# A two-layer decoder trunk on one core: q, k and two gate/up halves laid out with a gap, and the last pieces in two PSUM banks

## The chip, the core and the metric

The kernel runs on one core of a Trainium2 chip. The core has five engines that this document names as the profile does: PE (matrix multiply; its weight loads are shown as PEld), DVE (vector), ACT (scalar), POOL and SP. SP and ACT also issue the transfers between memory and the on-chip buffer SBUF; matrix results land in PSUM, which has eight banks. The metric is the time of one execution in microseconds, as the median of several runs.

## The reference

Two layers over 256 positions of width 1024, all in float32. Each layer is a token mixer (16 heads of 64; forgetting attention in layer 0, block attention with a learned relative bias in layer 1), a SwiGLU feed-forward of width 2816, and a gated per-layer input; a final RMSNorm gives the output of 256 x 1024.

```python
for i in range(DEPTH):                       # DEPTH = 2
    u = _rmsnorm(h, attn_norm_g[i])
    if i % 2 == 0:                           # forgetting attention
        proj = u @ fox_w_in[j]               # q, k, v and 16 gate columns
        ...
        o = _fox_attention(q, k, v, log_f)
        h = h + _merge_heads(o) @ fox_w_o[j]
    else:
        proj = u @ moba_w_in[j]              # q, k, v
        ...
        o = _moba_attention(q, k, v, rel_bias_table)
        h = h + _merge_heads(o) @ moba_w_o[j]
    u = _rmsnorm(h, ffn_norm_g[i])
    gu = u @ ffn_w_in[i]
    h = h + (jax.nn.silu(gu[..., :D_FF]) * gu[..., D_FF:]) @ ffn_w_out[i]
    gate = jax.nn.sigmoid(_rmsnorm(h, ple_norm_g[i]) @ ple_w_gate[i])
    h = h + gate * (p[i] @ ple_w_up[i])
return _rmsnorm(h, final_norm_g)
```

## The kernel before

**Weights come as halves.** The host cuts all weights into 216 "halves" of 128 x 1024 float32 (512 KB), in the order of their use, in the tensor `w`. `half` (L115) takes the next one: a transfer on SP's queue into a tile `raw` (six slots), a copy on ACT that rounds it to the PE's short float format (`whi`, L137), and a subtraction on DVE that leaves the rest (`wlo`, L138). `whi` and `wlo` are rings of six slots each. Every product is made of three matmuls (`mm3`, L80 to L84): high by high, high by low, low by high.

**Which operand is loaded.** In the products `pq` (q and k, `project`, L385) and `gu` (gate and up, `step` in `up`, L503), the half's blocks of 128 columns are the loaded weights and the activations `g` (tiles of `Norm`, high and low, 256 positions) are the moving operand. `blocks` (L141) cuts such a half into its eight blocks. In `v`, `wo`, `fo` and `pg` it is the other way round: activations are loaded, and a half is streamed in pieces of 512 columns.

**Places of the blocks.** A slot starts at a multiple of 64 elements (`LINE`). `blocks` puts the halves 16 elements behind that (`APART`). With `entry` set, `half` puts the first two blocks of the low part another 8 elements further (`FURTHER`), and the rest a `LINE` behind; this takes two subtractions (L129) instead of one. `up` asks for an entry for the gate's half of every even f from 4 on, and for the up half of f = 2 (L518).

**Order.** Each engine's instructions are put in order when the program is built. In `attention`, the j-th pair of heads goes through `project(j, 0)`, `scores(j - 1)` (`sp`), `transposes(j - 2)` (`pp`), `project(j, 1)` and `values(j - 2)` (`po`), so that a half of `pq` (24 matmuls) stands between other work. In `ffn`, f = 0 and 1 are done together over k, with the transposes `tp` of the second half of the residual between k = 2 and 3; then f = 2 with `spread` (`pr`) behind its first half; from f = 4 on, four halves (96 matmuls) follow on two halves of `fo` (`down`).

**The forget gate's weights.** In layer 0, `fox_bias` (L271) splits `wf32` into `fh` and `fl`, two tiles of their own of 4 KB per partition, zeroed once on POOL.

**The end.** In layer 1 `ple` (L596) closes with the final norm. The second half of the columns of `pg` (512 to 1023) is made for the first 128 positions (t = 0) with 512-wide matmuls, and for the last 128 (t = 1) in two pieces of 256 columns, both in one PSUM bank. Each piece goes through `part` (L644): a sigmoid on ACT, two DVE operations that add the gated input to `h`, and a square with its sum on ACT. For each t, POOL makes the scale from the sums (L670, L671); ACT scales the first 512 columns and sends them from its own queue, DVE finishes the other 512, and SP sends them. t = 0 is scaled and sent before t = 1's second piece.

```python
for i in range(2):
    for k in range(KT):
        c0 = (k % 2) * HC + i * S
        tokens(bks[1][t][:, i * S:(i + 1) * S], nm.k(k), t, ...)
    if i == 0:
        part(t, 0)
```

Of the kernel before, what the change touches and what calls it, by code (L numbers as in the profile page):

```python
# [32 lines left out]
P = 128  # L33
S = 256
# [23 lines left out]

ENTRY = 2
FURTHER = 8  # L60


@with_exitstack
def trunk(ctx: ExitStack, tc: tile.TileContext, x, xt, pt, w, wf, cst, pick, gains, gf, bf, rel, hot, rvm, out):
# [50 lines left out]
    def half(at=0, entry=0):  # L115


        i = state["next"]
        state["next"] += 1
        raw = work.tile([P, HW], F32, tag="raw", bufs=RAW, name=f"raw{i}")  # L120
        hi = work.tile([P, HW + LINE], F32R, tag="whi", bufs=6, name=f"whi{i}")[:, at:at + HW]
        lt = work.tile([P, HW + 2 * LINE], F32R, tag="wlo", bufs=6, name=f"wlo{i}")
        lo = lt[:, at:at + HW]
        if entry:
            nc.sync.dma_start(raw, w[i])
            nc.scalar.activation(hi, raw, AF.Copy)  # L126
            ats = [(at + FURTHER, 0, entry), (at + LINE, entry, HW)]
            for a, c0, c1 in ats:
                nc.vector.tensor_tensor(lt[:, a + c0:a + c1], raw[:, c0:c1], f32(hi[:, c0:c1]), op=ALU.subtract)  # L129
            return hi, [lt[:, a + k * P:a + (k + 1) * P] for a, c0, c1 in ats for k in range(c0 // P, c1 // P)]  # L130
        parts = 2 if i < 2 else 1
        for q in range(parts):
            c = slice(q * HW // parts, (q + 1) * HW // parts)
            if i == 0 and q == 1:
                nc.sync.dma_start(hx[:, 1], xt[:, 1])
            nc.sync.dma_start(raw[:, c], w[i][:, c])
            nc.scalar.activation(hi[:, c], raw[:, c], AF.Copy)  # L137
            nc.vector.tensor_tensor(lo[:, c], raw[:, c], f32(hi[:, c]), op=ALU.subtract)  # L138
        return hi, lo

    def blocks(entry=False):  # L141

        hi, lo = half(APART, ENTRY * P if entry else 0)
        hi = [hi[:, k * P:(k + 1) * P] for k in range(KT)]
        return hi, lo if entry else [lo[:, k * P:(k + 1) * P] for k in range(KT)]

# [95 lines left out]
    for t in (fh, fl):  # L242
        nc.gpsimd.memset(f32(t)[:, :, :, H:], 0.0)

    def split(hi, lo, src):
# [25 lines left out]
    def fox_bias(nm):  # L271


        split(fh[:, :, :, 0:H], fl[:, :, :, 0:H], wf32.unsqueeze(2).to_broadcast([P, KT, 4, H]))
        pf = bank("pf")
# [59 lines left out]
    def attention(layer, nm, mid, early, nf):  # L335
# [159 lines left out]
    def ffn(layer, nm, filler, np_):  # L495
# [3 lines left out]
        def up(fs):  # L499
# [96 lines left out]
    def ple(layer, nm, ut, nx):  # L596

        def gate(bk, t, c0, c1):
            at = slice(c0, c1)
            sg = work.tile([P, HC], F32, tag="t2k", bufs=3, name=f"pgt{layer}_{t}_{c0}")[:, 0:c1 - c0]  # L600
            nc.scalar.activation(sg, bk[:, c0 % HC:(c1 - 1) % HC + 1], AF.Sigmoid, scale=nm.col[:, t:t + 1])
            nc.vector.tensor_tensor(sg, sg, ut[:, t, at], op=ALU.mult)
            nc.vector.tensor_tensor(h[:, t, at], h[:, t, at], sg, op=ALU.add)

        bks = [[bank(f"pg{layer}_{hf}_{t}") for t in range(2)] for hf in range(2)]
# [26 lines left out]
        def square(t, i, c0, c1):  # L632

            sq = work.tile([P, HC], F32, tag="t2k", bufs=3, name=f"sqf{t}_{i}")
            nc.scalar.activation(sq[:, 0:c1 - c0], h[:, t, c0:c1], AF.Square, scale=D ** -0.5,
                                 accum_out=ss[:, t, i:i + 1])
# [7 lines left out]
        def part(t, i):  # L644
            c0 = HC + i * S
            gate(bks[1][t], t, c0, c0 + S)
            square(t, 1 + i, c0, c0 + S)
            if i == 0:
                nc.vector.tensor_tensor(ms[:, t, 1:2], ms[:, t, 0:1], ss[:, t, 1:2], op=ALU.add)
                nc.vector.tensor_tensor(ys[:, t, HC:HC + S], h[:, t, HC:HC + S], gb[:, HC:HC + S], op=ALU.mult)  # L650

        def rows(t, c0, c1, queue):
            queue.dma_start(out[t * P:(t + 1) * P, c0:c1], ys[:, t, c0:c1])

        for t in range(2):
            if t == 0:
                for c in range(4):
                    pair_unit(bks[1], c, wts[c], nm.k, (t,))
                part(t, 0)
            else:  # L660
                for i in range(2):
                    for k in range(KT):
                        c0 = (k % 2) * HC + i * S
                        tokens(bks[1][t][:, i * S:(i + 1) * S], nm.k(k), t, [w[:, c0:c0 + S] for w in wts[k // 2]],
                               k == 0, k == KT - 1)
                    if i == 0:
                        part(t, 0)
            part(t, 1)
            r = col[:, t:t + 1]
            nc.gpsimd.tensor_tensor(r, ss[:, t, 2:3], ms[:, t, 1:2], op=ALU.add)  # L670
            nc.gpsimd.tensor_tensor(r, r, nhalf[:, 0:1], op=ALU.pow)  # L671
            nc.scalar.activation(ys[:, t, 0:HC], ys[:, t, 0:HC], AF.Copy, scale=r)
            rows(t, 0, HC, nc.scalar)
            nc.vector.scalar_tensor_tensor(ys[:, t, HC + S:D], h[:, t, HC + S:D], r, gb[:, HC + S:D],
                                           op0=ALU.mult, op1=ALU.mult)
            nc.vector.tensor_scalar(ys[:, t, HC:HC + S], ys[:, t, HC:HC + S], r, None, op0=ALU.mult)
            rows(t, HC, D, nc.sync)

    for layer in range(2):
# [8 lines left out]
        nm = Norm(3) if layer == 0 else None  # L688
        ple(layer, np_, got[0], nm)


# [93 lines left out]
```

## Time and profile before

| | us |
|---|---|
| median of 3 runs | 674.04 (673.87 to 674.23) |
| the profiled execution's own time | 674.86 |
| its span, first to last instruction | 673.0 |
| PE busy in the span | 661.4 |
| DVE busy | 453.2 |
| ACT busy | 385.8 |
| mean granted clock of PE | 0.997 |

Times in the profile count from the first instruction. Matmuls overlap in the records (one is shown with its whole way through the array), so the time that one takes up on PE is read from the start of one to the start of the next. `gu<-g,whi` reads: the tile `gu` is written from `g` and `whi`; `L82` is the line of the program; `x704` counts instructions. A name after `<-` in square brackets is what ended an idle time. An arrow in the list of waits reads "waited for".

### The profile page before, as it was taken

Reading aid. Unit: us, or ns where it says so; the run is one execution under the profiler, and the core shown is the slowest. Engines: PE = TensorE matmul, PEld = TensorE weight load, DVE = VectorE, ACT = ScalarE, POOL = GpSimd, SP = SyncE. Lnnn points to the kernel's source line nnn. Section 1 sums busy time; section 2 is a strip of 40 time slices with the busy share of each in tenths; the row PEclk is TensorE's granted clock in tenths of the full one; section 3 lists DMA queues with packets and bytes.
Section 4 is the critical chain, followed back from the end, with each engine's and each line's share of the span. In section 5 each row is a group of like instructions: output and inputs, shape, how many; then the busy total and the mean of one; then the engine's idle time right before and its main releaser. Section 6 shows DMA issues by size and latency. Waiting matters only on the chain.

```text
span 673.0 us, 11820 instructions
## 1 busy us (share of the span) xinstructions
PE 661.4 (98%) x4620; PEld 607.0 (90%) x4620; DVE 453.2 (67%) x804; ACT 385.8 (57%) x697; POOL 10.0 (1%) x26
## 2 busy tenths in 40 slices
PE   8999999999999999999999999999999999999994
PEld 6889998999999999998889999889999999999884
DVE  5688775676666666666676888765766666666673
ACT  6876675564444444547666766655544444454663
POOL 2000000000000000000000000000000000000000
PEclk9999999999999999999999999999999999999998
DMA  8976334456555556555585533353755555565401
GB/s 277 384 279 237 126 127 129 153 170 207 193 196 195 199 188 208 193 197 174 185 286 199 172 127 126 107 175 107 241 195 193 197 197 188 188 212 195 173 1 62
DMA packets 37063, 123.78 MB, mean 184 GB/s; under 512 B 4288, under 2 KB 7056, under 8 KB 37008
## 3 DMA queue, kind: packets, MB, share of 16 engines
q1 hardware_dynamic: 36128, 121.35, 53.3%
q10 hardware_dynamic: 848, 1.68, 0.7%
q8 instruction: 36, 0.59, 0.3%
q14 instruction: 19, 0.16, 0.1%
q0 software_dynamic: 32, 0.01, 0.0%
HBM read 121.94 MB, written 4.22 MB: 187 GB/s over the span
## 4 chain that ended last, share of the span: by engine, by line
PE 92%; DMA 3%; ACT 2%; DVE 1%; issue 1%; SPq 0%; POOLq 0%; DVEq 0%; POOL 0%; ACTq 0%
PE gu L83 12%; PE gu L82 12%; PE gu L84 12%; PE fo L83 6%; PE fo L82 6%; PE fo L84 6%; PE pq L82 4%; PE pq L84 4%; PE pq L83 4%; DMA raw<-w 2%; PE wo L82 2%; PE wo L84 2%; PE wo L83 2%; PE pg L82 2%; PE pg L84 2%; PE pg L83 2%
## 5 line engine op out<-in xcount | busy, mean ns | idle before, releaser
L138 DVE TENSOR_TENSOR wlo<-raw,whi 128x1024 fp32r<-128x1024 f32 (+1 forms) x198 | 239.7, 1214 | 141.1 <-ACT whi L137 140.9
L137 ACT ACTIVATE whi<-raw 128x1024 fp32r<-128x1024 f32 (+1 forms) x198 | 207.2, 1050 | 159.3 <-PE gu L83 46.7
L82 PE MATMUL gu<-g,whi 128*128 128x256 f32 x704 | 195.5, 278 | 0.0
L84 PE MATMUL gu<-g,wlo 128*128 128x256 f32 x704 | 195.1, 277 | 0.0
L83 PE MATMUL gu<-g,whi 128*128 128x256 f32 x704 | 195.1, 277 | 0.0
L82 PEld LDWEIGHTS gu<-g,whi 128*128 128x128 f32 x704 | 132.6, 188 | 0.8
L83 PEld LDWEIGHTS gu<-g,whi 128*128 128x128 f32 x704 | 132.3, 188 | 0.7
L84 PEld LDWEIGHTS gu<-g,wlo 128*128 128x128 f32 x704 | 132.2, 188 | 0.0
L82 PE MATMUL pq<-g,whi 128*128 128x256 f32 x256 | 73.9, 289 | 0.0
L84 PE MATMUL pq<-g,wlo 128*128 128x256 f32 x256 | 71.8, 280 | 0.0
L83 PE MATMUL pq<-g,whi 128*128 128x256 f32 x256 | 71.7, 280 | 0.0
L82 PE MATMUL fo<-whi,fh 128*128 128x512 f32 x176 | 68.9, 391 | 0.0
L83 PE MATMUL fo<-wlo,fh 128*128 128x512 f32 x176 | 68.7, 390 | 0.0
L84 PE MATMUL fo<-whi,fl 128*128 128x512 f32 x176 | 68.5, 389 | 0.0
L82 PEld LDWEIGHTS pq<-g,whi 128*128 128x128 f32 x256 | 48.1, 188 | 1.0 <-ACT vhi L373 0.6
L84 PEld LDWEIGHTS pq<-g,wlo 128*128 128x128 f32 x256 | 48.7, 190 | 0.0
L83 PEld LDWEIGHTS pq<-g,whi 128*128 128x128 f32 x256 | 48.4, 189 | 0.0
L246 ACT ACTIVATE fh<-sg 128x256 fp32r<-128x256 f32 x44 | 18.2, 418 | 48.5 <-DVE sg L533 48.5
L129 DVE TENSOR_TENSOR wlo<-raw,whi 128x256 fp32r<-128x256 f32 (+1 forms) x40 | 26.0, 688 | 22.8 <-ACT whi L126 22.8
L84 PEld LDWEIGHTS fo<-whi,fl 128*128 128x128 f32 x176 | 33.1, 188 | 7.1
L82 PEld LDWEIGHTS fo<-whi,fh 128*128 128x128 f32 x176 | 33.1, 188 | 6.3
L83 PEld LDWEIGHTS fo<-wlo,fh 128*128 128x128 f32 x176 | 33.1, 188 | 6.0
(146 smaller groups left out, 967.1 us busy)
## 6 DMA issues: line engine op xcount, KB each, us to landing
raw<-w SPq DMA_DIRECT2D x214, 512.0 KB, 3.3
d<-d SPq DMA_DIRECT2D x4, 768.0 KB, 7.8
bias<-d SPq DMA_DIRECT2D x4, 512.0 KB, 5.2
raw<-w SPq DMA_DIRECT2D x4, 256.0 KB, 5.2
h<-x ACTq DMA_DIRECT2D x2, 512.0 KB, 5.3
hx<-xt SPq DMA_DIRECT2D x3, 256.0 KB, 5.1
p<-pt SPq DMA_DIRECT2D x2, 256.0 KB, 3.5
end<-gf SPq DMA_DIRECT2D x1, 512.0 KB, 4.4
```

What stands on the lines that cost most here:

```text
L82: mm(o, ah, bh, start=start, stop=False, skip_group_check=True)
L83: mm(o, ah, bl, start=False, stop=False, skip_group_check=True)
L84: mm(o, al, bh, start=False, stop=stop, skip_group_check=True)
L129: nc.vector.tensor_tensor(lt[:, a + c0:a + c1], raw[:, c0:c1], f32(hi[:, c0:c1]), op=ALU.subtract)
L137: nc.scalar.activation(hi[:, c], raw[:, c], AF.Copy)
L138: nc.vector.tensor_tensor(lo[:, c], raw[:, c], f32(hi[:, c]), op=ALU.subtract)
L246: nc.scalar.activation(hi, src, AF.Copy)
```

## The change

- **Gap.** A new `gapped` makes a half whose first block is followed by 56 unused columns (`GAP` = 64 - 8). High and low part both start 24 elements behind the slot's start, so the first block lies 8 elements further than with `blocks`, and the other seven lie as with `blocks`, one `LINE` on. The host puts the gap into `w`, so one transfer, one copy and one subtraction of 1080 columns do it. All rows of `w` are 1080 columns long for that, and the other halves take the first 1024.
- **Where.** `gapped` is used in `project` for all but the first three halves of each layer; in `up` for the gate's half of f = 0, where block 3 (the first behind the transposes) is put first, and for the up half of f = 2. The entry of L518 stays for f = 4, 6, and so on.
- **Room.** The slots of `raw`, `whi` and `wlo` grow (`raw` and `whi` by 256 bytes per partition). `fh` and `fl` give up their own tiles and take a slot of the rings.
- **The end.** The two last pieces have a bank each (`pgl`). The halves of the last four `pg` products are laid 48 elements into their slots (`AHEAD`). Both pieces of each t are multiplied with the gain on DVE as they come. Row block t = 0 is scaled on ACT alone, in two parts placed behind the last sigmoid and the last square, and leaves as one transfer of 512 KB on SP's queue; for t = 1 ACT scales the first 512 columns and DVE the other 512, and each is sent as before.

```diff
+GAP = LINE - FURTHER
+WW = HW + GAP
+AHEAD = 48
...
+    def gapped(first=0):
+        i = state["next"]
+        state["next"] += 1
+        raw = work.tile([P, HW + LINE], F32, tag="raw", bufs=RAW, name=f"raw{i}")
+        at = slice(APART + FURTHER, APART + FURTHER + WW)
+        ht, lt = (work.tile([P, HW + 2 * LINE], F32R, tag=n, bufs=6, name=f"{n}{i}")[:, at] for n in ("whi", "wlo"))
+        nc.sync.dma_start(raw[:, 0:WW], w[i])
+        nc.scalar.activation(ht, raw[:, 0:WW], AF.Copy)
+        nc.vector.tensor_tensor(lt, raw[:, 0:WW], f32(ht), op=ALU.subtract)
+        cs = [bool(n) * GAP + n * P for n in (_entered(first).index(k) for k in range(KT))]
+        return [[t[:, c:c + P] for c in cs] for t in (ht, lt)]
...
-    fh, fl = (one.tile([P, KT, 4, 32], F32R, name=n) for n in ("fh", "fl"))
...
+        fh, fl = (work.tile([P, HW + 2 * LINE], F32R, tag=t, bufs=6, name=n)[:, 0:HW].rearrange(
+            "p (k r c) -> p k r c", k=KT, r=4) for n, t in (("fh", "whi"), ("fl", "wlo")))
...
         def project(j, a):
-            hi, lo = blocks()
+            hi, lo = gapped() if 2 * j + a > 2 else blocks()
...
-                wts = {f: (blocks(), blocks()) for f in fs}
+                wts = {f: (blocks() if f else gapped(3), blocks()) for f in fs}
...
-                wt = blocks(a == 1 if fs[0] == 2 else a == 0 and fs[0] % 2 == 0)
+                if fs[0] == 2 and a:
+                    wt = gapped()
+                else:
+                    wt = blocks(ENTRY if fs[0] % 2 == 0 and a == 0 and fs[0] > 2 else ())
...
-        wts = [half() for _ in range(4)]
+        wts = [half(AHEAD) for _ in range(4)]
...
+        lb = (bks[1][1], bank("pgl"))
+        for i in range(2):
+            for k in range(KT):
+                c0 = (k % 2) * HC + i * S
+                tokens(lb[i][:, i * S:(i + 1) * S], nm.k(k), 1, [w[:, c0:c0 + S] for w in wts[k // 2]],
+                       k == 0, k == KT - 1)
+            last = part(1, i, lb[i])
+
+        for ins, c in zip(last, (slice(0, HC), slice(HC, D))):
+            with tc.issue_after(ins.ins):
+                nc.scalar.activation(ys[:, 0, c], ys[:, 0, c], AF.Copy, scale=col[:, 0:1])
+        rows(0, 0, D, nc.sync)
+        nc.scalar.activation(ys[:, 1, 0:HC], ys[:, 1, 0:HC], AF.Copy, scale=col[:, 1:2])
+        rows(1, 0, HC, nc.scalar)
+        nc.vector.tensor_scalar(ys[:, 1, HC:D], ys[:, 1, HC:D], col[:, 1:2], None, op0=ALU.mult)
+        rows(1, HC, D, nc.sync)
...
+def _entered(first):
+    return [first] + [k for k in range(KT) if k != first]
+
+def _gapped(a, first=0):
+    t = a.reshape(P, KT, P)[:, _entered(first)].reshape(P, HW)
+    return np.concatenate([t[:, :P], np.zeros((P, GAP), t.dtype), t[:, P:]], axis=1)
...
+        seq += qk[:3] + [_gapped(a) for a in qk[3:]]
...
+        a[0], a[5] = _gapped(a[0], 3), _gapped(a[5])
...
-    w = np.ascontiguousarray(np.stack(seq))
+    w = np.stack([np.pad(a, ((0, 0), (0, WW - a.shape[1]))) for a in seq])
```

More of the change, by code (lines that the diff above doesn't have):

```diff
@@ L119, in half @@
         state["next"] += 1
[L120 to L123, printed above, removed]
+        raw = work.tile([P, HW + LINE], F32, tag="raw", bufs=RAW, name=f"raw{i}")
+        ht, lt = (work.tile([P, HW + 2 * LINE], F32R, tag=n, bufs=6, name=f"{n}{i}") for n in ("whi", "wlo"))
+        hi, lo = ht[:, at:at + HW], lt[:, at:at + HW]
         if entry:
-            nc.sync.dma_start(raw, w[i])
-            nc.scalar.activation(hi, raw, AF.Copy)
+            nc.sync.dma_start(raw[:, 0:HW], w[i][:, 0:HW])
+            nc.scalar.activation(hi, raw[:, 0:HW], AF.Copy)
             ats = [(at + FURTHER, 0, entry), (at + LINE, entry, HW)]
@@ L139, in half, with blocks @@
         return hi, lo
[L141 to L145, printed above, removed]
+    def blocks(entry=()):
+        hi, lo = half(APART, len(entry) * P)
+        return [[t[k] if isinstance(t, list) else t[:, k * P:(k + 1) * P] for k in range(KT)] for t in (hi, lo)]
+    def gapped(first=0):
+        i = state["next"]
+        state["next"] += 1
+        raw = work.tile([P, HW + LINE], F32, tag="raw", bufs=RAW, name=f"raw{i}")
+        at = slice(APART + FURTHER, APART + FURTHER + WW)
[5 more added lines that the diff above has]
+        return [[t[:, c:c + P] for c in cs] for t in (ht, lt)]
     class Norm:
@@ L641, in ple, with part @@
             nc.vector.tensor_tensor(ys[:, t, 0:HC], h[:, t, 0:HC], gb[:, 0:HC], op=ALU.mult)
[L642 to L644 removed]
+        wts = [half(AHEAD) for _ in range(4)]
+        def part(t, i, bk):
             c0 = HC + i * S
[L646 to L647 removed]
+            got = gate(bk, t, c0, c0 + S), square(t, 1 + i, c0, c0 + S)
             if i == 0:
                 nc.vector.tensor_tensor(ms[:, t, 1:2], ms[:, t, 0:1], ss[:, t, 1:2], op=ALU.add)
[L650 removed]
+            nc.vector.tensor_tensor(ys[:, t, c0:c0 + S], h[:, t, c0:c0 + S], gb[:, c0:c0 + S], op=ALU.mult)
+            if i == 1:
+                r = col[:, t:t + 1]
+                nc.gpsimd.tensor_tensor(r, ss[:, t, 2:3], ms[:, t, 1:2], op=ALU.add)
+                nc.gpsimd.tensor_tensor(r, r, nhalf[:, 0:1], op=ALU.pow)
+            return got
@@ L652, in rows @@
         def rows(t, c0, c1, queue):
             queue.dma_start(out[t * P:(t + 1) * P, c0:c1], ys[:, t, c0:c1])
[L655 to L677, printed above, removed]
@@ new lines, in ple @@
+        for c in range(4):
+            pair_unit(bks[1], c, wts[c], nm.k, (0,))
+        for i in range(2):
+            part(0, i, bks[1][0])
+        lb = (bks[1][1], bank("pgl"))
+        for i in range(2):
+            for k in range(KT):
[6 more added lines that the diff above has]
+                nc.scalar.activation(ys[:, 0, c], ys[:, 0, c], AF.Copy, scale=col[:, 0:1])
```

17 lines of the change are left out of this document (9 added, 8 removed).

## The prediction

> **What bounds the kernel now.** I read the page first (busy shares and the chain that ended last), then what PE waited for, then single matmuls in the timeline.
>
> ```profile
> span 673.0 us, 11820 instructions
> ...
> PE 661.4 (98%) x4620; PEld 607.0 (90%) x4620; DVE 453.2 (67%) x804; ACT 385.8 (57%) x697; POOL 10.0 (1%) x26
> ...
> PE 92%; DMA 3%; ACT 2%; DVE 1%; issue 1%; SPq 0%; POOLq 0%; DVEq 0%; POOL 0%; ACTq 0%
> ```
>
> ```profile
> PE v L82 <- ACT g L159: 1.4, 1, 1.4
> ```
>
> PE is busy 98% of the span and 92% of the chain. The list of what PE waited for has two long entries: this one at the start, and one of the same length in the last pieces (its row stands at the tail, below). So time comes only from shorter matmuls, from that second wait, or from the tail behind the last matmul.
>
> Matmuls overlap in the records, so I read their cost as start to start. Four groups of 256-wide matmuls (`gu` and `pq`), each by a row near its start and its last one:
>
> ```profile
> 157.06 0.28 PE L82 MATMUL gu<-g,whi 128*128 128x256 f32 x1
> ...
> 167.15 0.28 PE L84 MATMUL gu<-g,wlo 128*128 128x256 f32 x1
> ```
>
> ```profile
> 132.18 0.28 PE L83 MATMUL gu<-g,whi 128*128 128x256 f32 x1
> ...
> 141.84 0.28 PE L84 MATMUL gu<-g,wlo 128*128 128x256 f32 x1
> ```
>
> ```profile
> 35.32 0.28 PE L82 MATMUL pq<-g,whi 128*128 128x256 f32 x1
> ...
> 42.68 0.28 PE L84 MATMUL pq<-g,wlo 128*128 128x256 f32 x1
> ```
>
> ```profile
> 78.38 0.28 PE L83 MATMUL pq<-g,whi 128*128 128x256 f32 x1
> ...
> 80.97 0.28 PE L84 MATMUL pq<-g,wlo 128*128 128x256 f32 x1
> ```
>
> The first pair is 89 matmuls apart: 10.09 / 89 = 113.4 ns each. The second: 9.66 / 82 = 117.8 ns. The third: 7.36 / 65 = 113.2 ns. The fourth: 2.59 / 22 = 117.7 ns. The same operation has two paces, 4.4 ns apart, with the granted clock at 1.00 in both (the windows below), and a group of such matmuls in a row keeps the pace that it enters with. The groups at the fast pace are the 18 of `gu` from f = 4 on (whose first half has the shifted entry of L127) and the first three halves of `pq` in each layer. At the slow pace are the other 13 halves of `pq` in each layer, and `gu` for f = 0 to 3. Those are the halves that the change lays out anew. How a group gets in:
>
> ```profile
> 156.35 0.28 PE L82 MATMUL gu<-g,whi 128*128 128x256 f32 x1
> ...
> 156.59 0.28 PE L84 MATMUL gu<-g,wlo 128*128 128x256 f32 x1
> 156.71 0.28 PE L82 MATMUL gu<-g,whi 128*128 128x256 f32 x1
> 156.83 0.28 PE L83 MATMUL gu<-g,whi 128*128 128x256 f32 x1
> 156.95 0.28 PE L84 MATMUL gu<-g,wlo 128*128 128x256 f32 x1
> ```
>
> ```profile
> 142.31 0.36 PE L82 MATMUL gu<-g,whi 128*128 128x256 f32 x1
> 142.52 0.28 PE L83 MATMUL gu<-g,whi 128*128 128x256 f32 x1
> 142.64 0.28 PE L84 MATMUL gu<-g,wlo 128*128 128x256 f32 x1
> 142.75 0.28 PE L82 MATMUL gu<-g,whi 128*128 128x256 f32 x1
> ```
>
> Behind `fo`, with the low half's first two blocks 8 elements further, the six steps from 156.35 to 157.06 take 0.71 us, 118 ns each, and only then does the pace drop. Behind the `pr` matmuls, the same shifted entry (the gate's half after f = 2's first) goes on at the slow pace to its end: the old form of entry fails there. So what precedes the group matters as well as the layout.
>
> **The change, part by part.**
>
> *Gap in `pq`.* In each layer 11 halves stand alone (24 matmuls), and one group has two halves (48). If the gap sets the fast pace after six matmuls without gain and one that cannot change, a lone half gains 17 x 4.4 = 75 ns, the pair 41 x 4.4 = 180 ns: 11 x 75 + 180 = 1.0 us per layer. *Gap in `gu`.* The group behind `tp` (84 matmuls) gains 77 x 4.4 = 0.34 us, the one behind `pr` (72) 65 x 4.4 = 0.29 us. Both layers: 2 x (1.0 + 0.63) = 3.3 us. The trace shows no group entered with both halves shifted, so this is bounded from both sides: 0 if nothing gets in, 3.3 if all does; below nothing, a shifted block inside a group at the fast pace (the second half of the pair) could throw it out, 24 x 4.4 = 0.1 us per layer. I take 3.3, nearest to the shifted entry that did work.
>
> *What the gap costs elsewhere.* A gapped half is 1080 columns instead of 1024, 5.5% more for ACT, DVE and the transfer.
>
> ```profile
> L138 DVE TENSOR_TENSOR wlo<-raw,whi 128x1024 fp32r<-128x1024 f32 (+1 forms) x198 | 239.7, 1214 | 141.1 <-ACT whi L137 140.9
> L137 ACT ACTIVATE whi<-raw 128x1024 fp32r<-128x1024 f32 (+1 forms) x198 | 207.2, 1050 | 159.3 <-PE gu L83 46.7
> ```
>
> With 1214 ns on DVE and 1050 on ACT that is 0.07 and 0.06 us for each of 30 halves. The shortest cover:
>
> ```profile
> 52.50:95.30 42.80, 42.80 (x381) 41.16 (x380) 34.09 (x106) 29.07 (x81) 0.00 (x0) 1.00 0.46 161
> 42.90:52.40 9.50, 8.81 (x78) 7.94 (x78) 7.87 (x21) 5.87 (x13) 0.00 (x0) 1.00 0.98 387
> 142.30:156.30 14.00, 14.00 (x99) 13.08 (x98) 12.75 (x21) 9.32 (x15) 0.00 (x0) 1.00 0.87 271
> ```
>
> (Columns: length, then busy time of PE, PEld, DVE, ACT, POOL; clock, DMA share, GB/s.) In attention DVE would have about 34.8 us of work in 42 us. From 142.3 it has 12.75 in 14.0, and there PE's gain is only 0.3 us; one split subtraction of f = 2 goes away too. Hidden, therefore nothing; if DVE were the bound there, the 0.3 us per layer would be lost.
>
> *The weights' rows.* All rows in memory lie 4320 bytes apart instead of 4096. Only where a transfer is waited for can that cost:
>
> ```profile
> 5.71 0.63 ACT L137 ACTIVATE whi<-raw 128x512 fp32r<-128x512 f32 x1 [3.04 <-DMA raw<-w]
> ...
> 6.79 0.80 PE L82 MATMUL v<-whi,g 128*128 128x512 f32 x1 [1.42 <-ACT g L159]
> ```
>
> The first conversion waits for its data, the first `g` stands behind it on ACT, and PE waits for that. Between 0 and 5.5% of the 3 us (as if each row carried its padding) is 0 to 0.2 us; I take +0.1. The Trainium skill ("DMA: Bandwidth & Descriptors", section "How a descriptor splits into AXI transactions") has a descriptor that doesn't start at a multiple of 256 B fetch from the boundary below it; 4320 is no multiple, so a 4096 B row would need on average some 3% more beats, an estimate that gives the same +0.1. No run here shows it yet.
>
> *`fh` and `fl` in the ring of halves.* Their slots are free at that point (four halves precede); the two memsets stay on POOL, which is busy 1% of the span: nothing.
>
> *Order.* The built program no longer pushes one `po` group into a half of `pq` in layer 1. By the starts of the transposes of successive j:
>
> ```profile
> 377.93 0.87 PE L443 MATMUL pp<-ident,e 128*128 128x128 f32 x6
> ```
>
> ```profile
> 386.56 0.87 PE L443 MATMUL pp<-ident,e 128*128 128x128 f32 x6
> ```
>
> ```profile
> 394.96 0.87 PE L443 MATMUL pp<-ident,e 128*128 128x128 f32 x6
> ```
>
> 8.63 us against 8.40: 0.2 us regained. `pr` moves six matmuls later in layer 0, and PE waits for nothing that hangs on it before: nothing.
>
> *The tail.*
>
> ```profile
> 660.82 0.28 PE L84 MATMUL pg<-whi,g 128*128 128x256 f32 x1
> ...
> 661.99 0.46 ACT L601 ACTIVATE pgt<-pg,col 128x256 f32<-128x256 f32 x1
> ...
> 662.50 0.39 PE L82 MATMUL pg<-whi,g 128*128 128x256 f32 x1 [1.40 <-ACT pgt L601]
> ...
> 663.06 0.72 ACT L672 ACTIVATE end<-end,colf 128x512 f32<-128x512 f32 x1 [0.62 <-POOL colf L671]
> ...
> 664.18 0.42 DVE L603 TENSOR_TENSOR h<-h,pgt 128x256 f32<-128x256 f32 x1
> ...
> 665.36 0.28 PE L84 MATMUL pg<-whi,g 128*128 128x256 f32 x1
> 665.67 0.47 ACT L601 ACTIVATE pgt<-pg,col 128x256 f32<-128x256 f32 x1 [0.52 <-PE pg L84]
> ...
> 668.54 0.72 ACT L672 ACTIVATE end<-end,colf 128x512 f32<-128x512 f32 x1 [0.94 <-POOL colf L671]
> ...
> 669.29 0.38 ACTq L653 DMA_DIRECT2D out<-end  x1
> ```
>
> With a second bank the last piece starts at 660.94 and its 24 matmuls (0.12 us each) end about 663.97 instead of 665.64. ACT must have done the first piece's square by then: sigmoid to 662.45, two DVE operations of 0.42 (no longer behind row 0's scaling at 663.06), square and read to about 663.95; it fits, with nothing over. From the sigmoid on the chain is 3.6 us as before: last issue about 667.6, 1.67 us earlier. Row 0's two scalings (0.72 each) go into ACT's waits behind the last sigmoid and the last square, ending about 666.7, just ahead of the last scale at 666.9. What is late next is the output: row 0 used to leave in two parts right behind the scale of 663.06, and now its 512 KB leave at 666.7, one microsecond ahead of the last 512 KB, on the same engines. At the 387 GB/s above 512 KB take 1.35 us, so the last bytes land about 0.45 us later than alone. Gain 1.2 us; between 0.7 (more queueing) and 1.67 (none).
>
> *Sum:* 3.3 + 0.2 + 1.2 - 0.1 = 4.6 us. The profiled execution took 674.86 us (span 673.0 and 1.9 around it), 0.8 above the median of 674.04: 670.2 for a profile, 669.4 us for the median.
>
> **The rivals.** *The gap sets the pace behind some predecessors only* (transposes but not `po`, or the reverse). The failure behind `pr` speaks for it; half of 3.3: 671.0 us.
>
> *The gap does nothing.* Then the tail and the order alone: 674.04 - 1.3 = 672.7 us, just at the edge of what a measurement of this kernel tells from no change (0.2%, 1.35 us). For it: in the trace the same entry works behind `fo` and not behind `pr`. Against it: two paces exist, and groups differ only in entry. The Trainium skill ("TensorE: Matmul & The Clock Gate", section "Step-by-step: what each phase is for") says that PE has two independent SBUF read ports and that loading the next weights takes nothing from the running matmul; by that rule the place of the weights could not matter, and the time is this rival's. Two paces of one operation at one clock do not fit it easily, but no run yet shows that the place is the cause.
>
> *The 18 groups of `gu` at the fast pace fall out of it*: the ending on the other side. All slots of `whi` grow by 256 bytes, `fh` shifts every later half by one slot of six, and `g` moves 8 KB. All 18 groups are entered from the same slot, so the trace cannot say that the slot doesn't matter. A lost group costs 89 x 4.4 = 0.39 us; from 12 lost groups on the gain is gone, all 18 cost 7.0 us: 676.4 us with the gap working, 679.7 without. Against it: a group at the fast pace goes on unchanged through all six slots, and lone slow halves have one pace in all slots.
>
> **How the numbers follow.** All of the gap works: 0.50 (669.4). Some of it: 0.16 (671.0). None: 0.19 (672.7, half of it within 0.2%). Lost `gu` runs: 0.10. Transfers that stall PE beyond the 0.1, or tail queueing with no gap: 0.05, within 0.2%. Faster 0.74, same 0.15, slower 0.11. The range goes from 668.0 (a tail of 1.67 and a gap entering at once) to 673.4 (nothing from the gap and 0.7 from the tail).
>
> **What would show it.** Right: lone `pq` halves 113 ns apart from about the seventh matmul; `gu` behind `tp` and `pr` likewise; no wait of `pg` for `pgt`; last issue about 5 us earlier. Wrong: 118 ns in `pq`, 118 ns in `gu` from f = 4 on, PE waiting for `wlo` near 142, or outputs landing over 3.5 us after their issue.

## The result, and the profile after

The changed kernel takes 671.28 us (median of 5 runs, 670.45 to 671.37) against 674.23 for the kernel before in the same comparison (673.87 to 674.53). The ratio is 0.9954 with an interval of 0.9939 to 0.9968: 2.95 us faster, where 4.6 were predicted. The profiled executions differ by more than the medians: 674.86 and 670.99 us, so 3.87. What follows is read from these two traces first; the difference between 3.87 and 2.95 is taken up at the end.

The page of the changed kernel, head and chain, and below it its whole list of what PE waited for:

```profile
span 669.2 us, 11816 instructions
...
PE 658.3 (98%) x4620; PEld 604.1 (90%) x4620; DVE 454.2 (68%) x801; ACT 386.5 (58%) x698; POOL 10.3 (2%) x26
...
PE 96%; DVE 1%; ACT 1%; DMA 1%; issue 0%; POOLq 0%; SPq 0%; POOL 0%; ACTq 0%
```

```profile
PE v L87 <- ACT g L175: 1.4, 1, 1.4
PE cold L106 <- PEq L811: 0.8, 1, 0.8
PE sp L428 <- DVE qkl L258: 0.7, 1, 0.7
```

PE now holds 96% of the chain instead of 92%, and the wait of the last `pg` for its `pgt` has gone from the list. Single matmuls show where the gap worked. The timeline of PE: a lone half of `pq` in layer 0, `gu` behind `tp` and behind `pr` in layer 0, in layer 1 the entry of one half of `pq` with its last matmul and the first of the same half for the next two j, and `gu` behind `tp`:

```profile
60.94 0.28 PE L88 MATMUL pq<-g,whi 128*128 128x256 f32 x1
...
63.54 0.28 PE L89 MATMUL pq<-g,wlo 128*128 128x256 f32 x1
...
132.00 0.28 PE L88 MATMUL gu<-g,whi 128*128 128x256 f32 x1
...
141.32 0.28 PE L89 MATMUL gu<-g,wlo 128*128 128x256 f32 x1
...
142.00 0.28 PE L88 MATMUL gu<-g,whi 128*128 128x256 f32 x1
...
149.96 0.28 PE L89 MATMUL gu<-g,wlo 128*128 128x256 f32 x1
...
377.64 0.36 PE L87 MATMUL pq<-g,whi 128*128 128x256 f32 x1
377.84 0.28 PE L88 MATMUL pq<-g,whi 128*128 128x256 f32 x1
377.96 0.29 PE L89 MATMUL pq<-g,wlo 128*128 128x256 f32 x1
378.08 0.28 PE L87 MATMUL pq<-g,whi 128*128 128x256 f32 x1
378.21 0.28 PE L88 MATMUL pq<-g,whi 128*128 128x256 f32 x1
378.32 0.28 PE L89 MATMUL pq<-g,wlo 128*128 128x256 f32 x1
...
380.36 0.28 PE L89 MATMUL pq<-g,wlo 128*128 128x256 f32 x1
...
385.85 0.36 PE L87 MATMUL pq<-g,whi 128*128 128x256 f32 x1
...
394.05 0.36 PE L87 MATMUL pq<-g,whi 128*128 128x256 f32 x1
...
455.14 0.28 PE L88 MATMUL gu<-g,whi 128*128 128x256 f32 x1
...
464.81 0.28 PE L89 MATMUL gu<-g,wlo 128*128 128x256 f32 x1
```

In layer 1 the half enters at steps of 0.12 and 0.13 us and drops at its sixth matmul: from 378.32 on it runs 18 steps in 2.04 us, 113.3 ns each. In layer 0 the same layout does nothing: 22 steps in 2.60 us, 118.2 ns. `gu` behind `tp` is at 113.7 ns in layer 0 (9.32 us for 82 steps) and at 117.9 in layer 1 (9.67), behind `pr` at 113.7 (7.96 for 70). The account between landmarks of the two traces, after less before:

| stretch | us |
|---|---|
| start of the first `pq` (34.51 to 34.55) | +0.03 |
| layer 0, `pq` and attention, to the first `gu` | -0.21 |
| layer 0, `gu` for f = 0 to 2 | -0.63 |
| from there to layer 1's first `pq` | 0.00 |
| layer 1, `pq` and attention, to the first `gu` | -1.36 |
| layer 1, from the first `gu` to the last `pg` products | -0.43 |
| the tail, from there to the end of the span | -1.25 |
| sum | -3.85 |

The -0.21 of layer 0 cannot be put down to the gap. Its stretch up to the nine slow halves (from j = 3's second half on) is 0.34 us shorter here, but it takes between 25.4 and 27.7 us in the traces below, with the gap or without. From the first of the nine on it is 0.12 us longer, because a half that does not get in pays for its slower entry steps.

PE's busy time is 3.1 us shorter (658.3 against 661.4). Of the 1.36 us, 0.23 are the `po` group that no longer breaks into a half: from one j to the next it is 8.21 and 8.20 us now (377.64, 385.85, 394.05), where before the one was 0.23 longer than the other. The tail, timeline of all engines:

```profile
658.33 0.28 PE L87 MATMUL pgl<-whi,g 128*128 128x256 f32 x1
...
660.93 0.28 PE L89 MATMUL pgl<-whi,g 128*128 128x256 f32 x1
...
661.34 0.46 ACT L620 ACTIVATE pgt<-pgl,col 128x256 f32<-128x256 f32 x1
...
661.70 0.71 ACT L693 ACTIVATE end<-end,colf 128x512 f32<-128x512 f32 x1
...
662.75 0.42 ACT L655 ACTIVATE sqf<-h 128x256 f32<-128x256 f32 x1 [0.34 <-DVE h L622]
...
663.16 0.70 ACT L693 ACTIVATE end<-end,colf 128x512 f32<-128x512 f32 x1
...
663.89 1.16 SPq L677 DMA_DIRECT2D out<-end  x2
664.19 0.72 ACT L695 ACTIVATE end<-end,colf 128x512 f32<-128x512 f32 x1 [0.32 <-POOL colf L673]
...
664.94 0.37 ACTq L677 DMA_DIRECT2D out<-end  x1
```

The last piece follows without a wait. From the last sigmoid (661.34) to the last issue (664.94) it is 3.60 us, as before. The two scalings of row 0 (661.70 and 663.16) lie in ACT's pauses and hold nothing up. The span ends 4.25 us behind the last issue on ACT's queue instead of 3.75: row 0's 512 KB went out 1.05 us ahead of it. The issues of the two pages, before and after, with the median time to the landing in the last column:

```profile
out<-end ACTq DMA_DIRECT2D x2, 256.0 KB, 2.7
```

```profile
out<-end ACTq DMA_DIRECT2D x1, 256.0 KB, 2.9
```

So the last landing is only 0.13 us later than before (2.87 and 2.74 us behind its issue in the traces). The other 0.37 us of the 0.50 pass between that landing and the last instruction of the program, 1.39 us instead of 1.02.

### The profile page after: what moved, and what is told of

The parts are those of the page before. It is cut to its first block, busy times and chain, and to the rows that moved or that the text cites. A ratio compares the mean times of both kernels' runs of the same rounds, so it can differ in the third digit from the quotient of the medians.

```text
span 669.2 us, 11816 instructions
## 1 busy us (share of the span) xinstructions
PE 658.3 (98%) x4620; PEld 604.1 (90%) x4620; DVE 454.2 (68%) x801; ACT 386.5 (58%) x698; POOL 10.3 (2%) x26
## 4 chain that ended last, share of the span: by engine, by line
PE 96%; DVE 1%; ACT 1%; DMA 1%; issue 0%; POOLq 0%; SPq 0%; POOL 0%; ACTq 0%
PE gu L89 12%; PE gu L88 12%; PE gu L87 12%; PE fo L87 6%; PE fo L88 6%; PE fo L89 6%; PE pq L87 4%; PE pq L88 4%; PE pq L89 4%; PE v L87 2%; PE v L88 2%; PE v L89 2%; PE wo L89 2%; PE wo L87 2%; PE wo L88 2%; PE pg L89 2%
## 5 line engine op out<-in xcount | busy, mean ns | idle before, releaser
L142 DVE TENSOR_TENSOR wlo<-raw,whi 128x1024 fp32r<-128x1024 f32 (+1 forms) x170 | 205.4, 1212 | 122.1 <-ACT whi L141 115.7
L141 ACT ACTIVATE whi<-raw 128x1024 fp32r<-128x1024 f32 (+1 forms) x170 | 177.3, 1047 | 138.4 <-PE gu L88 45.9
L159 DVE TENSOR_TENSOR wlo<-raw,whi 128x1080 fp32r<-128x1080 f32 x30 | 38.4, 1281 | 16.2 <-ACT whi L158 16.0
L158 ACT ACTIVATE whi<-raw 128x1080 fp32r<-128x1080 f32 x30 | 33.1, 1106 | 17.5 <-PE pq L88 7.5
L133 DVE TENSOR_TENSOR wlo<-raw,whi 128x256 fp32r<-128x256 f32 (+1 forms) x36 | 23.4, 688 | 22.7 <-ACT whi L130 22.7
```

The source lines that it names most:

```text
L158: nc.scalar.activation(ht, raw[:, 0:WW], AF.Copy)
L159: nc.vector.tensor_tensor(lt, raw[:, 0:WW], f32(ht), op=ALU.subtract)
```

## The experiments

Two theories stood against each other. The first: the pace of a group is set on entry, by how far the first block's place is moved against what stood before it on PE, and the change finds the right move only behind some predecessors. The second: the gap is not the cause, and the groups that became quicker owe it to the ring's new slots, to `g`'s new place, or to the longer rows. (Of the rings, `raw` and `whi` have larger slots; those of `wlo` keep their size.) The first four kernels undo one part or do one alone, and were timed together; before was at 674.51 us there.

**The gap undone, everything else kept.**

```diff
-            hi, lo = gapped() if 2 * j + a > 2 else blocks()
+            hi, lo = blocks()
...
-                wts = {f: (blocks() if f else gapped(3), blocks()) for f in fs}
+                wts = {f: (blocks(), blocks()) for f in fs}
...
-                    wt = gapped()
+                    wt = blocks()
...
-        seq += qk[:3] + [_gapped(a) for a in qk[3:]]
+        seq += qk
...
-        a[0], a[5] = _gapped(a[0], 3), _gapped(a[5])
```

> The changed kernel with the gap alone undone: the 30 gapped halves are laid as the others (1024 columns, 16 elements behind the slot's start); larger slots, fh and fl in the ring, rows 4320 bytes apart and the new tail stay. If the gap makes the faster pace: pq alone-standing halves and gu behind tp and pr back at 118 ns, and the time is that of before less the tail, 674.2 - 1.2 = 673.0 us (span about 671.9). If the moved slots and the ring made it: pq in layer 1 stays at 113 ns and the time at 671.3.

673.53 us, ratio 0.9987 (0.9978 to 0.9996). Its timeline of PE, a lone half in layer 1:

```profile
386.95 0.28 PE L88 MATMUL pq<-g,whi 128*128 128x256 f32 x1
...
389.54 0.28 PE L89 MATMUL pq<-g,wlo 128*128 128x256 f32 x1
```

It has 22 steps of 117.7 ns again, and so have all lone halves of layer 1 that stay whole; `gu` behind `tp` takes 9.98 us and behind `pr` 8.56, as before. The 18 groups from f = 4 on keep 10.91 us. So slots and rows neither help nor harm these groups, and the second theory falls. A plain group is not always slow, though: layer 0's pair of halves takes 5.65 us here, and 5.65 or 5.66 in the two kernels below that have no gap (the tail alone, the second bank alone), against 5.85 in the trace of before and 5.68 with the gap, and the 21 matmuls of the broken half are quick too. The broken half of `pq` is back too: the better order belongs to the gap, not to the ring.

**The gap alone, with the tail of before.**

```diff
-        wts = [half(AHEAD) for _ in range(4)]
+        wts = [half() for _ in range(4)]
...
-        lb = (bks[1][1], bank("pgl"))
```

(and `part`, `rows` and the loop over t as before)

> The changed kernel with the tail of before (one bank, row block 0 scaled and sent early, no AHEAD). If the parts add up: the changed kernel's 671.3 + 1.2 = 672.5 us, PE waiting 1.4 us in pg again; pq at 113 ns in all lone halves of layer 1 and only in the first two of layer 0, if the pace follows from the kernel and not from chance. If the pace is chance from run to run, other halves than these are at 113 ns.

672.19 us, ratio 0.9966 (0.9954 to 0.9978). The same halves are quick and slow as in the whole change: in layer 0 all nine from j = 3's second on at 2.92 and 3.02 us, in layer 1 all at 2.84 and 2.92. For these halves, what works where is therefore a property of the layout and the order, not chance.

**The tail alone, on the kernel before.**

```diff
-        wts = [half() for _ in range(4)]
+        wts = [half(AHEAD) for _ in range(4)]
...
+        lb = (bks[1][1], bank("pgl"))
...
+                nc.scalar.activation(ys[:, 0, c], ys[:, 0, c], AF.Copy, scale=col[:, 0:1])
+        rows(0, 0, D, nc.sync)
```

> The kernel before with the new tail alone. If the parts add up: 674.2 - 1.2 = 673.0 us; no wait of pg, the last transfer issued 1.7 us earlier, 0.5 us of it lost to the 512 KB of row block 0 just ahead of it. If the output queueing is dearer than read: 673.5 or more.

672.70 us, ratio 0.9972 (0.9961 to 0.9983), 1.8 us. In its trace the stretch from the last `pg` products to the end is 25.7 us, against 27.4 before and 26.1 in the whole change: the chain to the last issue is equally short in both (21.87 and 21.84 us), but here the span ends 3.81 us behind it, not 4.25. The transfers are the same and the last one lands 2.85 us behind its issue, as late as in the whole change; only the time from there to the end differs (0.96 against 1.39 us). What lengthens it there is not shown.

**The second bank alone**, without the new place of row 0 and without `AHEAD`.

```diff
+        lb = (bks[1][1], bank("pgl"))
...
-            gate(bks[1][t], t, c0, c0 + S)
+            gate(lb[i] if t else bks[1][0], t, c0, c0 + S)
...
-                        tokens(bks[1][t][:, i * S:(i + 1) * S], nm.k(k), t, ...
+                        tokens(lb[i][:, i * S:(i + 1) * S], nm.k(k), t, ...
```

> The kernel before with the second bank alone; row block 0 is scaled and sent where it was. PE no longer waits in pg, but the first piece's square on ACT still stands behind row block 0's scaling (square and its read end at 665.2 in the trace of before), so the last sigmoid can move only from 665.67 to about 665.2: 0.4 to 0.5 us gained, 673.8 us. If the bank alone is what counts: 1.4 us or more, 672.8.

673.83 us, ratio 0.9991 (0.9982 to 1.0). Its timeline:

```profile
663.60 0.72 ACT L674 ACTIVATE end<-end,colf 128x512 f32<-128x512 f32 x1 [0.62 <-POOL colf L673]
...
665.18 0.42 ACT L635 ACTIVATE sqf<-h 128x256 f32<-128x256 f32 x1 [0.86 <-DVE h L603]
...
665.60 0.46 ACT L601 ACTIVATE pgt<-pgl,col 128x256 f32<-128x256 f32 x1
```

The matmuls are done at 664.5, but the last sigmoid stands on ACT behind the first piece's square, and that behind DVE and row 0's scaling. Only 0.68 us of the 1.4 us wait come back in the medians (by the interval, between 0 and 1.2), and 0.63 in the traces. The wait that goes is replaced by one on ACT; moving row 0 is the other half of the tail's gain. And `AHEAD` has a part: these 23 steps of `pgl` take 120.0 ns, with `AHEAD` 113.3, 0.15 us. The piece before it gains 0.13 in the same way, and the last 24 of the 512-wide matmuls ahead of both lose 0.16 (233 ns instead of 227), so `AHEAD` is worth 0.13 us in all.

Now the question was why layer 0's nine halves stay slow. The first theory says: what stands before them. In layer 0 the scores have extra matmuls, which add the forget gate's bias. One kernel leaves them out.

**Without the forget gate's matmuls in the scores.**

```diff
         bias, add = rest()
+        add = None
```

> The changed kernel without the forget-gate matmuls that layer 0 adds to its scores (so layer 0's attention ignores the forget gate and its mask is all that is added; 16 matmuls left out, the output is not the reference's). Layer 0's stretch of pq is then matmul for matmul that of layer 1. If those matmuls set the phase that the gap misses: all lone halves of layer 0 at 113 ns, some 0.7 us gained beyond the matmuls left out. If a group inherits the pace of the group before it: layer 0 stays at 118 ns from the fourth lone half on.

Its timeline, the half that took 118.2 ns in the changed kernel:

```profile
60.32 0.28 PE L88 MATMUL pq<-g,whi 128*128 128x256 f32 x1
...
62.84 0.28 PE L89 MATMUL pq<-g,wlo 128*128 128x256 f32 x1
```

Run once, it took 668.70 us. The half has 2.52 us for 22 steps, the same as layer 1's 377.84 to 380.36. All nine are quick (2.84 and 2.92 us with their ends). And `gu` turned over with them: now the first 36 of layer 0 are quick and the 84 behind `tp` slow (9.99 us), as in layer 1. With not one weight moved, what ran before decided.

**One half of layer 1 plain again** (j = 3's second).

```diff
-            hi, lo = gapped() if 2 * j + a > 2 else blocks()
+            hi, lo = gapped() if 2 * j + a > 2 and (layer, j, a) != (1, 3, 1) else blocks()
```

> The changed kernel with one half of layer 1 (pair j = 3, k) laid plainly, without the gap. If each group finds its pace at its own entry: that half runs at 118 ns and the eight lone halves behind it at 113 ns as before; 0.08 us lost. If a slow group makes the next ones slow, as layer 0's row of slow halves could be read: all behind it at 118 ns, 0.7 us lost.

```profile
386.23 0.28 PE L88 MATMUL pq<-g,whi 128*128 128x256 f32 x1
...
388.82 0.28 PE L89 MATMUL pq<-g,wlo 128*128 128x256 f32 x1
...
390.21 0.28 PE L88 MATMUL pq<-g,whi 128*128 128x256 f32 x1
...
392.82 0.28 PE L89 MATMUL pq<-g,wlo 128*128 128x256 f32 x1
...
394.64 0.28 PE L88 MATMUL pq<-g,whi 128*128 128x256 f32 x1
...
397.17 0.28 PE L89 MATMUL pq<-g,wlo 128*128 128x256 f32 x1
```

Run once, it took 671.34 us. The plain half is slow (117.7 ns), the gapped one that follows it behind `po` is slow too (118.6), and the next, behind the scores and transposes, is quick (2.53 us). So with this layout the pace passes through a `po` group, and is set anew behind scores and transposes. In the same trace layer 1's pair of halves starts at the slow pace and turns quick behind the shifted block of its second half: a shifted block inside a group can bring it in.

**All eight blocks 8 elements further, without a gap.**

```diff
+    def further():
+        return [[t[:, k * P:(k + 1) * P] for k in range(KT)] for t in half(APART + FURTHER)]
...
-            hi, lo = gapped() if 2 * j + a > 2 else blocks()
+            hi, lo = further() if 2 * j + a > 2 else blocks()
```

> The changed kernel with the 13 halves of pq in each layer laid 24 elements behind the slot's start throughout: all blocks 8 further, no gap. If the change of place behind the first block makes the pace: no lone half at 113 ns, 2 us lost against the changed kernel at most. If the place itself is what counts (8 elements further is better for all blocks): every lone half at 113 ns in both layers, 0.7 us gained.

```profile
386.85 0.28 PE L88 MATMUL pq<-g,whi 128*128 128x256 f32 x1
...
389.46 0.28 PE L89 MATMUL pq<-g,wlo 128*128 128x256 f32 x1
```

Run once, it took 672.57 us. The rows are a lone half of layer 1, where the gap works: 118.6 ns. The lone halves take 117.2 to 118.9 ns a step in both layers, no better than plain. The place as such is no cure; in layer 1 the step between first block and rest was.

**Other steps in layer 0's nine halves.** `laid(nhi, nlo, d)` puts the first `nhi` blocks of the high part and `nlo` of the low part `d` elements further, the rest a `LINE` on.

```diff
+    LAID = {(3, 1): (0, 2, 8), (4, 0): (0, 2, 8), (4, 1): (2, 2, 8), (5, 0): (2, 2, 8), (5, 1): (1, 1, 4),
+            (6, 0): (1, 1, 4), (6, 1): (1, 1, 12), (7, 0): (1, 1, 12), (7, 1): (1, 0, 8)}
...
-            hi, lo = gapped() if 2 * j + a > 2 else blocks()
+            hi, lo = (laid(*LAID[j, a]) if layer == 0 and (j, a) in LAID else gapped() if 2 * j + a > 2 else blocks())
```

> The changed kernel with other layouts for the nine lone halves of layer 0 from j = 3, k on: two blocks of the low part 8 further (j = 3 k, j = 4 q), two blocks of both parts 8 further (4 k, 5 q), one block of both 4 further (5 k, 6 q), one block of both 12 further (6 k, 7 q), one block of the high part 8 further (7 k). If the pace depends on the phase at entry and on how far the shifted blocks move it: some of these at 113 ns, others at 118. If something else in layer 0 forbids the faster pace: all nine at 118 ns.

| layout of the first blocks | behind `pp` | behind `po` |
|---|---|---|
| low part, two blocks, 8 | 118 ns | 118 |
| both parts, two blocks, 8 | 118 | 118 |
| both parts, one block, 4 | 118 | 113 |
| both parts, one block, 12 | 113 | 113 |
| high part, one block, 8 | 113 | not tried here |

(Each is the middle step of its half.) The row of 4 in the timeline, behind `pp` and then behind `po`:

```profile
77.15 0.29 PE L88 MATMUL pq<-g,whi 128*128 128x256 f32 x1
...
79.75 0.28 PE L89 MATMUL pq<-g,wlo 128*128 128x256 f32 x1
...
81.14 0.28 PE L88 MATMUL pq<-g,whi 128*128 128x256 f32 x1
...
83.64 0.28 PE L89 MATMUL pq<-g,wlo 128*128 128x256 f32 x1
```

Run once, this kernel took 669.49 us. The two halves have 2.60 us and 2.50 us for 22 steps each; here the second got in although the one ahead of the `po` group was slow, so the pace is not always handed on. Two layouts found their way in behind `pp`, where 8 on both parts fails. The next two kernels use one each for all nine.

**12 in place of 8 for the nine; `gu`'s first half in layer 1 plain.**

```diff
-    def gapped(first=0):
+    def gapped(first=0, d=FURTHER):
...
-            hi, lo = gapped() if 2 * j + a > 2 else blocks()
+            hi, lo = blocks() if 2 * j + a < 3 else gapped(0, 12 if layer == 0 and 2 * j + a > 6 else FURTHER)
...
-                wts = {f: (blocks() if f else gapped(3), blocks()) for f in fs}
+                wts = {f: (gapped(3) if f == 0 and layer == 0 else blocks(), blocks()) for f in fs}
```

> The changed kernel with the first block of layer 0's last nine lone halves (from j = 3, k on) 12 elements further instead of 8, and with layer 1's gate half of f = 0 laid plainly. If the shift must fit the phase that the forget-gate matmuls leave: all nine at 113 ns, 9 x 0.08 = 0.7 us gained; if the two at 12 in the mixed run owed it to the half before them: some of the nine at 118. In layer 1, where the first 36 matmuls of gu are at 113 ns and the 84 behind the transposes at 118: if the gap breaks what was in pace, the plain half leaves all 84 at 113 ns, 0.34 us gained; if the transposes alone decide, 118.

```profile
464.29 0.28 PE L88 MATMUL gu<-g,whi 128*128 128x256 f32 x1
...
472.54 0.28 PE L89 MATMUL gu<-g,wlo 128*128 128x256 f32 x1
```

All nine halves of layer 0 are quick (2.83 and 2.94 us with their ends, where the changed kernel has 2.92 and 3.02). Run once, it took 670.12 us. The rows are `gu` behind `pr` in layer 1. In layer 1 `gu` behind `tp` stayed slow, and with it the gapped group behind `pr` (8.25 us for 70 steps, 117.9 ns), which was quick in the changed kernel: here too one unchanged layout changes its pace with what precedes it.

**The high part alone for the nine, 12 for layer 1's `gu`, and row 0 sent in two parts.**

```diff
-            hi, lo = gapped() if 2 * j + a > 2 else blocks()
+            hi, lo = laid(1, 0, FURTHER) if layer == 0 and 2 * j + a > 6 else gapped() if 2 * j + a > 2 else blocks()
...
-                wts = {f: (blocks() if f else gapped(3), blocks()) for f in fs}
+                wts = {f: (blocks() if f else gapped(3, 12 if layer else FURTHER), blocks()) for f in fs}
...
-        rows(0, 0, D, nc.sync)
+            rows(0, c.start, c.stop, nc.sync)
```

> The changed kernel with the first block of the high part alone 8 further in layer 0's last nine lone halves, with 12 instead of 8 for layer 1's gate half of f = 0, and with row block 0 of the output sent in two parts, each behind its scaling. Phase must fit: the nine all at one pace behind the transposes (113 ns in the mixed run) and all at one pace behind po (not seen yet). The 84 of layer 1: 113 ns if 12 fits that phase. Tail: the first 256 KB leave 1.4 us earlier, so the last transfers queue behind half as much; 0.3 us gained from the last pg matmul to the end, none if issuing one more transfer costs as much.

```profile
60.73 0.28 PE L88 MATMUL pq<-g,whi 128*128 128x256 f32 x1
...
63.24 0.28 PE L89 MATMUL pq<-g,wlo 128*128 128x256 f32 x1
...
453.80 0.28 PE L88 MATMUL gu<-g,whi 128*128 128x256 f32 x1
...
463.12 0.28 PE L89 MATMUL gu<-g,wlo 128*128 128x256 f32 x1
...
663.25 0.38 ACTq L703 DMA_DIRECT2D out<-end  x1
```

Run once, it took 668.78 us. Every group is now at the quick pace but layer 0's first 36 `gu`, whose layout is plain (117.8 ns): the nine at 2.50 or 2.51 us, `gu` behind `tp` in layer 1 at 9.32 us for 82 steps (9.67 in the changed kernel). The span ends 3.75 us behind the last issue instead of 4.25, and the last transfer lands 2.4 us behind its issue instead of 2.9: row 0 in one transfer had held it up. This version was timed beside the changed kernel.

> The kernel of e10_high_only once more, timed. If the pace of each group follows from the layout: again every lone half of pq and the 84 and 72 matmuls of gu at 113 ns in both layers, and 1.6 us less than the changed kernel in the same call (0.8 in layer 0's pq, 0.34 in layer 1's gu, 0.5 in the tail): about 669.5 us, 0.7% under the kernel before. If it was chance: some groups at 118 ns and no steady difference.

> The changed kernel itself beside it. If the pace follows from the layout: layer 0's last nine lone halves at 118 ns and layer 1's all at 113 again; 671.3 us as on record, between 0.9 and 4 us over or under it by the start (34 us before pq begins), which differs from run to run.

The new version takes 668.79 us (668.6 to 670.3), ratio to before 0.9921 (0.9908 to 0.9933); the changed kernel takes 670.97, ratio 0.9948 (0.9934 to 0.9961), with before at 674.30. So a further 2.2 us below the change. Between their two traces, 2.46 us apart, 1.08 lie between the first of the nine halves and layer 0's first `gu` (0.89 in the halves, the rest in the `po` groups and scores between them), 0.16 in layer 1's `gu` and 0.53 in the tail. The other 0.7 lie ahead of the nine halves, where traces with the same layout up to there lie up to 1 us apart (60.73 to 61.69 us for the start of the first of the nine). In the changed kernel's second trace layer 1's first 36 `gu` are slow and the 84 behind `tp` quick (9.64 us), the other way round than in its first: the pace behind `wo` differs between executions of one kernel. Over all traces the gap of 8 got in behind `tp` wherever the 36 before were slow (ten groups) and failed wherever they were quick (seven); the gap of 12 got in where they were quick (two).

## Why the prediction was right, and where it was wrong

*What bounds the kernel, and the two paces:* right. PE had no long wait to lose but the one in the tail, and most of the rest of the gain came from matmuls at 113 instead of 118 ns. The Trainium skill ("TensorE: Matmul & The Clock Gate", section "Step-by-step: what each phase is for") gives PE two independent read ports and says that a weight load takes nothing from the running matmul. What the prediction drew from it for a rival, that the place of the weights could not matter, is contradicted here: gap alone 672.19 against 674.51 us, and 113.3 against 117.7 ns for one half with the weights laid differently. Whether the ports are the reason is not shown. With that the rival "the gap does nothing" (672.7) falls.

*The gap's term, 3.3 us:* this is the step that failed. It measures 2.4: layer 0's `pq` 0.21 instead of 1.0, and that in a stretch that varies by more (its nine failing halves lose 0.12); layer 0's `gu` 0.63, as predicted to the hundredth; layer 1's `pq` 1.13 instead of 1.0; layer 1's `gu` 0.43 instead of 0.63, its 84 behind `tp` unchanged, with 0.15 from the first 36, which were quick in this execution and not in the second one traced. In layer 1 the halves gained just what was predicted: 0.07 or 0.08 us each against 0.075, and 0.17 for the pair against 0.18. They drop after five steps and not seven, but three steps of the entry take 118 to 124 ns. What came on top are the `po` groups between them, whose 256-wide matmuls go on at the quick pace (a group has 1.04 us instead of 1.07), a term that the prediction didn't have.

The prediction saw that an entry can fail behind one predecessor (`pr`) and still took the upper bound for all, "nearest to the shifted entry that did work". It counted kinds of neighbour, not layers: the same neighbours' names, `pp` and `po`, lead into the same layout in both layers, and it works in one alone. The layer's extra matmuls are the difference, as the kernel without them shows. The rival "the gap sets the pace behind some predecessors only", 671.0 us, is what happened, though not divided as it said, transposes here and `po` there.

*The 18 groups of `gu`:* right, no group fell out; 10.91 us for each in both traces and with the ring alone.

*Cover of ACT and DVE:* right, no new wait of PE for `whi` or `wlo` is on the list above.

*The weights' rows, +0.1:* this cannot be told from nothing. By the issues of the pages, the median landing of an unpadded half is 3.5 us here and 3.6 with the gap undone. In the kernels with rows 4096 bytes apart it is 3.3 (before), 3.4 (the tail alone) and 3.5 us (the second bank alone). So these traces neither bear out nor contradict the Trainium skill's rule on descriptors that begin off a 256 B boundary ("DMA: Bandwidth & Descriptors", section "How a descriptor splits into AXI transactions"). The prediction's estimate of 3% from it stays untested. PE's first `pq` came 0.03 us later, but it starts between 33.53 and 36.23 us over all traces, before and changed layouts mixed, so a term of 0.1 cannot be told there either.

*Order, 0.2:* 0.23. *The tail, 1.2:* 1.25, by its own steps: the last issue came 1.75 us earlier counted from the last `pg` products (1.67 predicted, and `AHEAD`, which had no term, gives 0.13), and the end behind it took back 0.50 us (0.45 predicted). The second size is right in part by luck. Queueing behind row 0's one transfer is real: sent in two parts, the last landing comes 0.45 us sooner after its issue. But against before, where two transfers of 256 KB left together at the end, the landing is only 0.13 us later. The other 0.37 us lie behind the landing, and the tail alone, with the same transfers, does not have them; their cause stays open.

*Profile against median:* the terms add to 3.85 us, and the two profiled executions differ by just that (3.87). The medians differ by 2.95, and by 3.33 in the second timing. The profiled execution of before lay 0.6 us above its median and that of after 0.3 below; the start (2.7 us between traces) and layer 0's stretch up to the nine halves (2.3 us between traces), with the pace of its first halves, which varies with an unchanged layout, are large enough for it. Some 0.3 us of the 3.85 may thus not be the gap's: layer 0's pair (0.17) is also quick in other traces without the gap, and layer 1's first 36 `gu` (0.15) were not quick in the changed kernel's second trace. Which of them it was in executions without a trace stays open. Open too is whether ring and rows cost something: the kernel without the gap gained 1.0 us where the tail alone gained 1.8, but the intervals (0.9978 to 0.9996 and 0.9961 to 0.9983) overlap, and in the traces 0.42 us of the difference lie behind the last landing (1.38 against 0.96).

## What to carry to other kernels

When one operation shows two durations at one clock, look at how its groups begin, and price a new entry for each place by the work that precedes it there, down to the layer: a layout that gets one group into the quick pace is a trial elsewhere, not a rule. Look at several executions before you call a group slow: a few changed pace with nothing changed in their layout. Several forms of entry can be tried in one run, one for each of several equal groups, and read off the starts of the matmuls. A wait that is taken away in a tail is worth only what the next engine in line lets through: the second bank alone gave back about half, and of the 1.75 us by which the last issue came earlier the end of the program took back 0.50.

## What the runs showed of the hardware

- A 128x128 by 128x256 matmul of this kernel, each with its own weights, goes at 113.3 to 113.7 or at 117.7 to 118.2 ns, at 117.2 to 118.9 with the blocks all 8 further, and at 120.0 in `pgl` without `AHEAD`. The granted clock does not explain it: it is 1.00 at both paces. The pace is taken on within some five matmuls and, with one layout throughout, held to the end of the group. With the gap of 8 it was carried through the `po` matmuls, and set anew behind scores and transposes.
- What sets it is the move of the first block or blocks against the rest, together with what ran before: behind the same transposes of layer 0, 4 and 8 on both parts fail, 12 on both and 8 on the high part alone get in. Which property of the memory or of PE lies behind this was not tried.
- The pace of the same group behind `wo` differed between two executions of one unchanged kernel (layer 1's first 36 `gu`), and a plain pair of halves in layer 0 took 5.85 us in the trace of before and 5.65 or 5.66 in two other kernels that have the same layout there.
- With their halves laid 48 elements into the slot, 512-wide matmuls of `pg` went from 227 to 233 ns, and 256-wide ones from 120 to 113.
